# The first pass of a two-layer attention kernel: another way to spread c, another order of its side work, more buffers

## The chip, the cores and the metric

The kernel runs on one core of a Trainium2 chip. The metric is the device time in microseconds (us) of one execution. The engines are TensorE (PE, with its weight loads listed apart as PEld), VectorE (DVE), ScalarE (ACT), GpSimd (POOL) and SyncE (SP). SP issues every transfer of this kernel, in one queue, in order; all transfers run on 16 shared DMA engines. Each engine works through its own instructions in the order in which the program was laid out, and waits for semaphores of the others.

## The reference

The reference is an encoder of two layers over 1024 tokens of width 1024. Each layer normalizes x, scales and shifts it by values that come from a vector c, projects it, attends, gates and adds. What matters here is the start of layer 0:

```python
mod = jax.nn.silu(c) @ ada_w + ada_b
shift, scale, gate = jnp.split(mod[:, None, :], 3, axis=-1)
h = _rmsnorm(x, norm_g[0]) * (1.0 + scale) + shift
proj = h @ w_in
q, k, v, z = jnp.split(proj, [DA_WIDTH, 2 * DA_WIDTH, 3 * DA_WIDTH], axis=-1)
q = _rope(q, positions); k = _rope(k, positions)
```

`_rope` needs the sines and cosines of positions times 32 frequencies. All products are kept near float32: each operand is split into a high part (float32r) and the rest, and three products are added (`mm3`).

## The kernel before, in words

Tokens come in 8 tiles of 128, and the 1024 features in 8 chunks of 128. The **first pass** takes the first 512 tokens (tiles 0 to 3, `xs0`), chunk by chunk (the loop over `k` at L610). For a chunk it needs three things.

- The modulation of the 128 features: shift (`modb`) and scale (`moda`) are dot products of silu(c) with rows of `ada_ss0`. `load_c` (L421) loads c into all 128 partitions with one broadcast transfer, ACT makes tanh (L427), DVE makes 2 silu(c) (L428), and ACT copies it to the PSUM tile `cb` (L559). A chunk has two `ada` tiles of 512 KB (`ada0`, L561) and two DVE products with sums (`mod_dot`, L434); L442 makes `moda` final. Four `ada` buffers go round (`ADA_B`).
- The transposed chunk of x. ACT and DVE take the squares of the four tiles (`sq_x`, L527), one `inv_rms` (L465, with a power on POOL at L171) serves all four, and then the tiles are scaled in place: the first 256 columns on ACT (L567), the other 768 on DVE (L621), behind the first modulation. `h_chunk` (L479) lets PE transpose the four 128x128 blocks (L488), ACT writes `h0h` (L493) and the unrounded `h` (L495), POOL writes the rest `h0l` (L498).
- The split weights of v: `load_wv` (L542) fetches `wvr`, ACT rounds it (L547), POOL takes the rest (L548). Each four chunks there is also a strip of the weights of k (`wk0`, split in `split_raw`, L229 and L230). A strip waits in one of two `wraw` buffers.

PE then runs 15 products of 128x512 for the chunk (L638 to L644): 12 for four v accumulators (`vacc`), 3 for the first k accumulator (`kacc`). With `SKEW` 1 the transposes of the next chunk stand among them. Amid the last chunks the x of tokens 512 to 1023 (`xs1`) and the first strips of q (`wq0`) are loaded, after `ada` of chunk 7. Behind the last modulation stand `angles` (L572): ten DVE instructions and three sines on ACT, whose results go to DRAM (`tabS`, L594) and come back as `cosT` and `sinT` (L599).

After the pass come the q product of the first half (`qacc`, L648) and `store_v` (L359), which splits a v accumulator into a `v_hl` buffer (two of them, `VB`) and sends it to DRAM; only then is its PSUM bank free. Then the **second half** of the tokens follows with the same weights, then k and q of head 0, the second half of v's columns (`v0_tile`), and the attention. During these, DVE also works off the modulation of layer 1 (`gen_mods`, L453), with `ada` tiles that SP loads between the others.

The order on each engine is laid out by a scheduler from the program's order and its own estimates; `tc.issue_after(ins)` pins what a block issues behind `ins` on that engine.

Of the kernel before, what the change touches and what calls it, by code (L numbers as in the profile page):

```python
# [60 lines left out]
VB = (2, 3)  # L61
# [3 lines left out]
WQ_AT = 6  # L65
# [3 lines left out]
X_CUT = 256  # L69
FIN_LAG = 1  # L70
# [15 lines left out]
def trunk(ctx: ExitStack, tc: tile.TileContext, A, out):  # L86
# [329 lines left out]
    def mod_load(src, mp, nb, tag="ada"):  # L416
        w = mp.tile([P, D], F32, name="ada", tag=tag, bufs=nb)
        SP.dma_start(w, src)
        return w

    def load_c(pl, th, **kw):  # L421

        c2 = pl.tile([P, D], F32, name="c2", **kw)
        SP.dma_start(c2, A["c"].to_broadcast([P, D]))

        def fin():
            S.activation(th, c2, AF.Tanh, scale=0.5)  # L427
            V.scalar_tensor_tensor(out=c2, in0=th, scalar=1.0, in1=c2, op0=ALU.add, op1=ALU.mult)  # L428

        return c2, fin  # L430
# [48 lines left out]
    def h_chunk(l, xn4, k, dst, hp, sub=G, wide=False, act=False, f32=None):  # L479
# [13 lines left out]
        S.activation(hh, tr[:, :n, :], AF.Identity, bias=bk, scale=ak)  # L493
        if act:
            S.activation(tmp, tr[:, :n, :], AF.Identity, bias=bk, scale=ak)  # L495
# [18 lines left out]
    def load_x(half):  # L514

        xs = []
        for j in range(4):
            if half == 1 and j > 1:
                xs.append([wp.tile([P, HF], F32, name="xth", tag="rp", bufs=6) for _ in range(2)])
            else:  # L520
                xs.append([p1.tile([P, D], F32, name="xt", tag="xt", bufs=6)])
            for i, x_ in enumerate(xs[j]):
                n = D // len(xs[j])
                SP.dma_start(x_, A["x"][half * 4 + j, :, i * n : i * n + n])
        return xs

    def sq_x(xs, on_act=range(4)):  # L527
        ss = sm.tile([P, 4], F32, name="xss")
        for j, x_ in enumerate(xs):
            for i, piece in enumerate(x_):  # L530
                dst = ss[:, j : j + 1] if i == 0 else sm.tile([P, 1], F32, name="xs2")
                if j in on_act:
                    junk = p1.tile([P, D], BF16, name="junk", tag="junk", bufs=1)
                    S.activation(junk[:, : piece.shape[1]], piece, AF.Square, accum_out=dst)
                else:
                    junk = p1.tile([P, D], BF16, name="junk2", tag="h32", bufs=2)
# [24 lines left out]
    def ada0(j):  # L561
        return [mod_load(A["ada_ss0"][j, i], p1, ADA_B) for i in range(2)]
# [1280 lines left out]
```

## Time and profile before

| what | us |
|---|---|
| three runs, median (lowest to highest) | 1440.93 (1437.67 to 1443.14) |
| the profiled execution, its own time | 1438.65 |
| its span, first to last instruction | 1436.9 |
| PE busy in the span | 1388.8 |
| DVE, ACT, POOL busy | 917.5, 728.7, 610.6 |

The span leaves 1.75 us of the profiled execution's time outside. A row of the timeline gives the start, the duration, the engine, the line, the operation, output and inputs, sizes and count, and in brackets the idle time of the engine before it with what ended it. Rows of several instructions are merged (x4). The end of a PE product is modelled and overlaps the start of the next: the pace of PE is read from starts. A row of the windows gives, for a stretch, its length and the busy time and count of PE, PEld, DVE, ACT and POOL, then the granted PE clock (1.00 is full), the share of the DMA engines in use and their GB/s. A row of waits gives who waited for whom, the total, the times, and the longest.

### The profile page before, as it was taken

The numbers are of one execution on the slowest core, as the hardware profiler recorded it, in microseconds if no ns is written. First come the engines' busy times: TensorE is split into PE (matmuls) and PEld (weight loads), VectorE is DVE, ScalarE is ACT, GpSimd is POOL, SyncE is SP. The second block draws the span as 40 slices with busy tenths as digits, with TensorE's granted clock in tenths as the row PEclk, the third lists the DMA queues.
The fourth block names the chain that finished last, engine by engine and source line by source line (L and its number), as shares of the span: only waits on it lengthen the run. The fifth ranks groups of instructions, "written<-read, shape, count | busy, mean of one in ns | idle before, by whom it ended". The sixth has DMA issues, their size and how long they took to land. (4 is left out here: it accounts for less than half of the span.)

```text
span 1436.9 us, 20644 instructions
## 1 busy us (share of the span) xinstructions
PE 1388.8 (97%) x7388; PEld 1158.8 (81%) x7388; DVE 917.5 (64%) x1372; ACT 728.7 (51%) x1287; POOL 610.6 (42%) x483
## 2 busy tenths in 40 slices
PE   5999999999999999998999999999999999999997
PEld 4778788888888888887787877887888888888886
DVE  6656877767777767677435985545666555555355
ACT  5622375666565656566343452335455554545342
POOL 4416164656464646464461343532141331412572
PEclk9999999999999999999999999999999999999999
DMA  8787723333332333237653145398343432336563
GB/s 326 238 254 237 255 70 93 84 104 81 96 101 84 96 89 91 86 96 248 236 183 125 38 132 184 122 305 236 133 130 111 130 101 77 104 96 217 185 237 136
DMA packets 135527, 213.70 MB, mean 149 GB/s; under 512 B 19072, under 2 KB 56064, under 8 KB 135424
## 3 DMA queue, kind: packets, MB, share of 16 engines
q1 hardware_dynamic: 135424, 212.38, 47.1%
q8 instruction: 58, 0.95, 0.3%
q14 instruction: 45, 0.37, 0.1%
HBM read 137.92 MB, written 50.80 MB: 131 GB/s over the span
## 5 line engine op out<-in xcount | busy, mean ns | idle before, releaser
L384 ACT CAST pth<-tr 128x512 fp32r<-128x512 f32 x256 | 150.6, 588 | 284.2 <-PE tr L382 281.9
L399 DVE TENSOR_REDUCE nm<-s 128x1 f32<-128x1024 f32 x192 | 234.1, 1219 | 77.2 <-PE s L773 65.7
L385 DVE TENSOR_TENSOR ptl<-tr,pth 128x512 fp32r<-128x512 f32 x256 | 176.2, 688 | 139.4 <-ACT pth L384 138.9
L230 POOL TENSOR_TENSOR wl<-wraw,wh 128x512 fp32r<-128x512 f32 (+2 forms) x79 | 103.6, 1314 | 205.6 <-ACT wh L229 183.4
L401 ACT ACTIVATE e<-s,nm 128x1024 f32<-128x1024 f32 x128 | 143.7, 1123 | 29.8 <-DVE nm L399 29.2
L382 PE MATMUL tr<-ident,e 128*128 128x128 f32 x1024 | 155.1, 274 | 2.3 <-DVE ptl L385 2.0
L382 PEld LDWEIGHTS tr<-ident,e 128*128 128x128 f32 x1024 | 121.2, 140 | 43.6 <-DVE ptl L385 19.2
L184 PE MATMUL acc<-h0h,wh 128*128 128x512 f32 x360 | 150.1, 417 | 1.9 <-DVE v_hl L362 1.8
L184 PE MATMUL pv<-pth,vt 128*128 128x256 f32 x512 | 147.1, 287 | 0.0
L185 PE MATMUL pv<-ptl,vt 128*128 128x256 f32 x512 | 145.8, 285 | 0.0
L186 PE MATMUL pv<-pth,vt 128*128 128x256 f32 x512 | 144.7, 283 | 0.0
L186 PE MATMUL acc<-h0h,wl 128*128 128x512 f32 x360 | 143.1, 398 | 0.5 <-POOL wl L230 0.5
L185 PE MATMUL acc<-h0l,wh 128*128 128x512 f32 x360 | 142.0, 394 | 0.0
L1013 POOL TENSOR_TENSOR wol<-wor,woh 128x512 fp32r<-128x512 f32 x64 | 85.0, 1351 | 84.7 <-ACT woh L1012 77.2
L185 PEld LDWEIGHTS pv<-ptl,vt 128*128 128x128 f32 x512 | 97.6, 191 | 2.9
L184 PEld LDWEIGHTS pv<-pth,vt 128*128 128x128 f32 x512 | 97.4, 190 | 2.9 <-ACT pth L384 0.2
L186 PEld LDWEIGHTS pv<-pth,vt 128*128 128x128 f32 x512 | 97.6, 191 | 0.1
L326 POOL TENSOR_TENSOR rp_r<-rp_raw,cosT 128x512 f32<-128x512 f32 x38 | 49.8, 1311 | 91.0 <-ACT rp_raw L321 50.8
L331 POOL TENSOR_TENSOR rp_sw<-rp_sw,sinT 128x512 f32<-128x512 f32 x42 | 55.4, 1318 | 74.1 <-DMA rp_sw<-rp_raw 73.9
L773 PE MATMUL s<-ks,qa 128*128 128x512 f32 x256 | 82.6, 404 | 2.8 <-DVE e L781 2.6
L781 DVE SCALAR_TENSOR_TENSOR e<-s,z,e 128x1024 f32<-128x1024 f32 x64 | 82.1, 1283 | 2.1
L773 PE MATMUL s<-ks,qb 128*128 128x512 f32 x256 | 81.1, 395 | 0.0
(590 smaller groups left out, 3335.4 us busy)
## 6 DMA issues: line engine op xcount, KB each, us to landing
ada<-in_ada_ss SPq DMA_DIRECT2D x32, 512.0 KB, 6.0
wraw<-in_w_s SPq DMA_DIRECT2D x64, 256.0 KB, 2.9
vS<-v_hl SPq DMA_DIRECT2D x32, 512.0 KB, 5.9
vt<-vS SPq DMA_DIRECT2D x32, 512.0 KB, 3.7
wor<-in_w_out SPq DMA_DIRECT2D x64, 256.0 KB, 3.9
rp_sw<-rp_raw SPq DMA_DIRECT2D x168, 64.0 KB, 2.0
bc_s<-bc_d SPq DMA_DIRECT2D x34, 256.0 KB, 4.1
oS<-bc_s SPq DMA_DIRECT2D x30, 256.0 KB, 2.5
```

The lines of the kernel that those rows point to most:

```text
L184: PE.matmul(psum, ah, bh, start=first, stop=False)
L185: PE.matmul(psum, ah, bl, start=False, stop=False)
L186: PE.matmul(psum, al, bh, start=False, stop=last)
L230: sub = (V if pair_of else G).tensor_sub(l_[:, :n], raw[:, :n], f32v(h_[:, :n]))
L382: PE.transpose(tr[:, j, :], p[:, kt * P : (kt + 1) * P], ident)
L384: mk["S"] = S.copy(pth[kh][:, :, dst], tr).ins
L385: mk["V"] = V.tensor_sub(ptl[kh][:, :, dst], tr, f32v(pth[kh][:, :, dst])).ins
L399: mk["V"] = V.reduce_max(nm, s_ps, axis=AX.X, negate=True).ins
L401: mk["S"] = S.activation(e, s_ps, AF.Exp, bias=nm, scale=1.0, accum_out=zs).ins
L773: PE.matmul(s_ps[:, kc * HF : (kc + 1) * HF], src[:, c, ql], KS[h][kc][:, c, :], start=fst, stop=not fst)
L781: combined.append(V.scalar_tensor_tensor(out=e0, in0=e1, scalar=z1[:, 0:1], in1=e0, op0=ALU.mult, op1=ALU.add).ins)
L1013: in_turn(G.tensor_sub(lo, raw, f32v(hi)))
```

## The change

- **c.** One row of c is loaded into one partition (`crow`); tanh and the product run on this partition; two float32 products of a row of ones with it write `cb`, spread over all partitions. `crow` and `th` both take `ada` buffers. `c2`, which the modulation of layer 1 needs in SBUF, is copied from `cb` amid chunk 5.
- **Products of ones.** Before the spread 8, and behind it 28 products of `ones` with itself (128x128, float32) are issued on PE into a bank of the `acc` rotation (`warm`), and not used.
- **Last token tile apart.** Squares, mean and scale of tiles 0 to 2 are made first; tile 3 has its own chain, with its squares half on ACT and half on DVE. DVE scales tiles 0 to 2 without being pinned behind the first modulation.
- **Angles and sines.** `positions` is loaded after the weights of chunk 1. The DVE steps of the angles stand in four parts behind the modulations of chunks 1 to 4, the sines behind `h_chunk` of chunks 4 and 5, the last two DVE steps and the transfers at chunk 6.
- **Order.** The splits of weights are pinned behind the `h` of the chunk before; the q strips are fetched one chunk earlier (`WQ_AT` 5), behind `ada` of chunk 6; `xs1` behind `ada` of chunk 7. Squares of `xs1`: the first two tiles on DVE, the other two on ACT.
- **Buffers.** `v_hl` of layer 0 has four buffers instead of two; `dynamic_dma_scratch_size` is 1024 instead of its default.

```diff
-VB = (2, 3)
+VB = (4, 3)
-WQ_AT = 6
+WQ_AT = 5
+WARM = (8, 28)
+SIN_AT = (4, 5, 6)
...
+    warm = bank("acc", "warm")
+    def keep_busy(n):
+        for _ in range(n):
+            PE.matmul(warm[:, 0:P], ones, ones, start=True, stop=True)
+    crow = p1.tile([P, D], F32, name="crow", tag="ada", bufs=ADA_B)
     th = p1.tile([P, D], F32, name="cth", tag="ada", bufs=ADA_B)
-    c2, c_fin = load_c(p1b, th)
-    xs0 = load_x(0)
+    SP.dma_start(crow[0:1, :], A["c"])
+    xs0 = [load_x(0, 0)]
+    xs0 += [load_x(0, j) for j in range(1, 4)]
+    keep_busy(WARM[0])
...
-    c_fin()
-    cb = bank("cb", "cb", [P, D])
-    S.copy(cb, c2)
...
+    c_act = S.activation(th[0:1, :], crow[0:1, :], AF.Tanh, scale=0.5).ins
+    c_last = V.scalar_tensor_tensor(out=crow[0:1, :], in0=th[0:1, :], scalar=1.0, in1=crow[0:1, :], op0=ALU.add, op1=ALU.mult).ins
+    cb = bank("cb", "cb", [P, D])
+    for f in range(2):
+        fs = slice(f * HF, f * HF + HF)
+        spread = PE.matmul(cb[:, fs], ones[0:1, :], crow[0:1, fs], start=True, stop=True).ins
+    with tc.issue_after(spread):
+        keep_busy(WARM[1])
...
-    y0 = inv_rms(sq_x(xs0, X_ACT0), 4)
+    y_ = inv_rms(ss0[:, 0:3], 3)
+    for j in range(3):
+        y0[j] = y_[:, j : j + 1]
+        S.mul(xs0[j][0][:, :X_CUT], xs0[j][0][:, :X_CUT], y0[j])
+    sq_halves([xs0[3][0][:, :HF], xs0[3][0][:, HF:]], ss0[:, 3:4])
+    y0[3] = inv_rms(ss0[:, 3:4], 1)[:, 0:1]
+    h_chunk.act = S.mul(xs0[3][0][:, :X_CUT], xs0[3][0][:, :X_CUT], y0[3]).ins
...
+    for j in range(3):
+        x_rest(j)
...
+    def sines(n):
+        with tc.issue_after(h_chunk.act):
+            if n == 0:
+                S.activation(kk, ang, AF.Sin, scale=0.5)
+                S.activation(nsin, ang, AF.Sin, scale=-1.0)
+            if n == 1:
+                S.activation(ang, ang, AF.Sin)
+                S.copy(c2, cb)
...
+            if k >= 0:
+                with tc.issue_after(m_last):
+                    next(angle_steps, None)
         if k < 0:
             with tc.issue_after(m_last):
-                for j in range(4):
-                    V.tensor_scalar(xs0[j][0][:, X_CUT:], xs0[j][0][:, X_CUT:], y0[:, j : j + 1], None, op0=ALU.mult)
-        if k == KT - 1:
-            with tc.issue_after(m_last):
-                angles()
+                x_rest(3)
         if k == X1_AT:
-            xs1 = load_x(1)
+            with tc.issue_after(mod_load.last):
+                xs1 = [load_x(1, j) for j in range(4)]
         if k == WQ_AT:
-            wq0 = load_strip([A["w_s0"][0, 0, f] for f in range(2)], [4, 4], None, ada_pair)
+            with tc.issue_after(mod_load.last):
+                qraw = fetch_strip([A["w_s0"][0, 0, f] for f in range(2)], [4, 4])
+            with tc.issue_after(h_chunk.act):
+                wq0 = split_strip(qraw, None, ada_pair)
             q_split = load_strip.last
         if 0 <= k < KT:
             h_chunk(0, xs0, k, h0[k][0], p1, act=True)
+            if k + 1 < KT:
+                with tc.issue_after(h_chunk.act):
+                    wv0.append(split_wv(vraw))
+            if k in SIN_AT:
+                sines(SIN_AT.index(k))
...
-    norm_x(sq_x(xs1), xs1)
+    ss1 = sm.tile([P, 4], F32, name="xss")
+    with tc.issue_after(m_last):
+        for j in range(2):
+            sq_piece(xs1[j][0], ss1[:, j : j + 1], False)
+    with tc.issue_after(h_chunk.act):
+        for j in range(2, 4):
+            sx = sm.tile([P, 1], F32, name="xs2")
+            sq_piece(xs1[j][0], ss1[:, j : j + 1], True)
+            sq_piece(xs1[j][1], sx, True)
+            V.tensor_add(ss1[:, j : j + 1], ss1[:, j : j + 1], sx)
+    norm_x(ss1, xs1)
...
-    nc = bacc.Bacc("TRN2", target_bir_lowering=False, num_devices=1)
+    nc = bacc.Bacc("TRN2", target_bir_lowering=False, num_devices=1, dynamic_dma_scratch_size=1024)
```

More of the change, by code (lines that the diff above doesn't have):

```diff
@@ L417, in mod_load @@
         w = mp.tile([P, D], F32, name="ada", tag=tag, bufs=nb)
-        SP.dma_start(w, src)
+        mod_load.last = SP.dma_start(w, src).ins
         return w
[L421 to L430, printed above, removed]
     def mod_dot(w, bias, acc, c_):
@@ L512, in trunk @@
     p1 = pool(st1, "p1a")
-    def load_x(half):
-        xs = []
-        for j in range(4):
[L518 to L536, printed above, removed]
-                    V.tensor_tensor_reduce(out=junk, in0=piece, in1=piece, scale=1.0, scalar=0.0, op0=ALU.mult, op1=ALU.add, accum_out=dst)
-                if i:
-                    V.tensor_add(ss[:, j : j + 1], ss[:, j : j + 1], dst)
-        return ss
```

106 lines of the change are left out of this document (76 added, 30 removed).

## The prediction

> **What bounds the kernel now.** I read the page first, then the waits of PE, then the timeline of the first 60 us, then windows.
>
> ```profile
> span 1436.9 us, 20644 instructions
> ```
>
> The waits of PE over the first 60 us:
>
> ```profile
> PE trh L488 <- ACT xt L567: 14.5, 1, 14.5
> PE vacc L643 <- POOL h0l L498: 2.1, 1, 2.1
> ```
>
> PE does not start before 14.5 us, and has one more long wait, near the end of the first pass. The kernel's time is that of PE, so what the first pass can give is this start, this wait, and what both cost in pace. The timeline of the start:
>
> ```profile
> 0.72 0.39 SPq L150 DMA_DIRECT2D vec<-in_vec  x1
> ...
> 1.17 0.42 SPq L424 DMA_DIRECT2D c<-in_c  x1
> ...
> 2.46 0.15 DVE L162 TENSOR_SCALAR g<-vec 128x1 f32<-128x1 f32 x1 [1.47 <-DMA vec<-in_vec]
> ...
> 6.22 1.06 ACT L427 ACTIVATE cth<-c 128x1024 f32<-128x1024 f32 x1 [4.22 <-DMA c<-in_c]
> 7.31 1.23 DVE L428 SCALAR_TENSOR_TENSOR c<-cth,c 128x1024 f32<-128x1024 f32 x1 [4.70 <-ACT cth L427]
> ...
> 10.08 1.06 ACT L534 ACTIVATE junk<-xt 128x1024 bf16<-128x1024 f32 x1 [0.49 <-DMA xt<-in_x]
> ...
> 11.23 1.23 DVE L537 CUSTOM_DVE_ANT_0 junk<-xt 128x1024 bf16<-128x1024 f32 x1 [1.22 <-DMA xt<-in_x]
> ...
> 12.57 0.17 DVE L466 TENSOR_SCALAR xss<-xss 128x4 f32<-128x4 f32 x1
> ...
> 12.87 1.28 DVE L434 CUSTOM_DVE_ANT_0 ada<-ada,cb,vec 128x1024 f32<-128x1024 f32 x1
> ...
> 15.52 4.26 DVE L621 TENSOR_SCALAR xt<-xt,rq_y 128x768 f32<-128x768 f32 x4
> ...
> 17.01 0.80 PE L638 MATMUL vacc<-wvh,h0h 128*128 128x512 f32 x1 [0.87 <-ACT h0h L493]
> ...
> 18.87 1.05 PE L488 MATMUL trh<-ident,xt 128*128 128x128 f32 x4
> ...
> 22.21 0.16 DVE L442 SCALAR_TENSOR_TENSOR moda<-moda,vec 128x1 f32<-128x1 f32 x1
> ...
> 23.30 0.50 PE L638 MATMUL vacc<-wvh,h0h 128*128 128x512 f32 x1 [0.18 <-ACT h0h L493]
> ```
>
> x of the third tile lands at 10.08, of the fourth at 11.23. From L466 at 12.57 DVE works without a gap until `moda` of chunk 1 at 22.37 (22.21 + 0.16), 9.8 us, and the products of chunk 1 follow at 23.30, 0.93 later. So chunk 1 is set by DVE; that chunk 0 runs at half pace (0.80 a product) hides behind that. From there PE runs on:
>
> ```profile
> 46.74 0.39 PE L638 MATMUL vacc<-wvh,h0h 128*128 128x512 f32 x1
> ...
> 48.78 0.39 PE L641 MATMUL kacc<-h0h,wl 128*128 128x512 f32 x1
> 51.28 1.93 PE L643 MATMUL vacc<-wvh,h0l 128*128 128x512 f32 x4 [2.10 <-POOL h0l L498]
> ...
> 53.73 0.79 PE L184 MATMUL acc<-h0h,wq 128*128 128x512 f32 x1
> ...
> 55.06 0.39 PE L184 MATMUL acc<-h0h,wq 128*128 128x512 f32 x1
> ```
>
> Six chunks from 23.30 to 46.74 are 3.91 us each. Of chunk 7 the first ten products took 2.04 (46.74 to 48.78), 0.227 each. Without the stall its 15 products would end at 50.15; the q product starts at 53.73, and its first three take 1.33 instead of 0.68. The stall costs 3.6 + 0.65 = **4.2 us**, twice its 2.1 of idle, since PE comes back slow. The windows show this in the granted clock:
>
> ```profile
> 50.00:55.00 5.00, 3.62 (x8) 2.37 (x9) 2.07 (x4) 3.84 (x11) 1.22 (x1) 0.66 0.71 213
> ```
>
> Why `h0l` was late stands on ACT: the table load of the sines and two sines stand between `h0h` and `h` of chunk 7.
>
> ```profile
> 47.20 1.28 ACT L588 ACT_TABLE_LOAD   x1
> ...
> 49.12 0.76 ACT L495 ACTIVATE h<-trh,modb,moda 128x512 f32<-128x512 f32 x1
> ```
>
> **The change part by part.** *The start.* The traffic in windows:
>
> ```profile
> 1.50:4.50 3.00, 0.00 (x0) 0.00 (x0) 0.15 (x1) 0.50 (x1) 0.00 (x0) 1.00 0.78 183
> ...
> 6.50:14.50 8.00, 0.04 (x1) 0.04 (x1) 5.50 (x9) 4.65 (x8) 1.04 (x1) 1.00 1.03 416
> ```
>
> The broadcast of c writes 524 KB (0.524 MB) and goes ahead of x. At the 416 GB/s of the second stretch that is 1.26 us; at the 183 of the first, where the DMA engines were in use for 0.78 of the time, 2.87. I take 2.2: the first stretch is where c moved, but some of it is the start itself. So x of tile 2 lands at 7.9, its squares end 1.15 later as before (10.08 to 11.23), at 9.05, and DVE's run may start there, since tile 3 no longer stands ahead: 3.5 earlier than 12.57. The run has the same two modulations and four scalings, and about 1.0 more for tile 3 (half of the 1.23 of L537, one addition, a second L466, an estimate from these rows), and up to 0.4 of waiting for the first `ada` tile. **Start: 3.5 - 1.0 - 0.4 = 2.1 us** (1.2 with 1.26 for c; 3.2 with 2.87 and no waiting). Whether DVE scales tiles 0 to 2 or makes the modulation first moves chunk 0, not chunk 1.
>
> That c itself is sooner: its row is issued at 1.17 and lands as `vec` did (issued 0.72, used 2.46), near 2.9; tanh 1.06 and the product 1.23 end near 5.4, not 8.54. PE spreads from 5.5. The trace has no such spread. The nearest are products of ones late in the kernel:
>
> ```profile
> 1350.48 1.05 PE L830 MATMUL rb<-dg,ones 128*128 128x128 f32 x8
> ```
>
> Four float32 products of the program stand here as 8 rows, so 0.26 us each at full pace; transposes at slow pace (18.87, 1.05 for 4) are twice as long a row, 0.52. The spread is 8 such widths: 2.1 to 4.2 us. The 28 products behind it are 7.4 to 14.7. They end at 15.0 at full pace (hidden: before, DVE was done with the modulation of chunk 0 at 15.5), and at 24.4 at slow pace. The transposes of chunk 0 stand behind them on PE, and ACT's `h0h`, POOL's `h0l` behind these. I take the fast end, because the first 8 products have by then kept PE at work from about 1 us; the slow end is a rival. TensorE: Matmul & The Clock Gate in the Trainium skill (Part 1) says that about 3.4 us of activity lifts the gate to full pace and an idle window takes it back; by that the 28 run fast. The trace agrees as far as it goes: PE is slow at 17.01 and 18.87, and at full pace for the chunks from 23.30 on. By the slow row alone the start would give nothing.
>
> With `crow` and `th` in `ada` buffers, the loads for chunk 1 wait for the spread's end; 416 GB/s of x and `ada` of chunk 0 are queued ahead, so 0.
>
> *Angles and sines.* DVE's steps cost what they did, now between modulations.
>
> ```profile
> 43.89 1.39 DVE L575 CAST ang<-posi 128x256 f32<-128x256 int32 x1
> ```
>
> A chunk has 2.7 of DVE (two of 1.28 and L442) in 3.91 us of PE, so later ones cover theirs. The cast stands between the modulations of chunks 1 and 2, when DVE is just ahead: 0 to 0.6 lost, I take 0.2. On ACT the table load and two sines come to 2.1 in one chunk; ACT's own work there is a rounding and two activations like L495's 0.76, about 2.2. 4.3 against 3.91 is 0.4 late at most, and I take 0: ten of a chunk's products (2.3 us) stand ahead of the first that needs `h0l`. The stall of 4.2 goes. ScalarE: Activation LUTs in the Trainium skill (What ACT_TABLE_LOAD costs) gives 2.66 us with a drain; the trace shows 1.28, with the sine at once behind it. By the page ACT would be 1.8 late and PE lose a few tenths.
>
> What is late next is `vacc`: the q product takes a bank that `store_v` must free, an ACT copy and a DVE subtraction:
>
> ```profile
> 52.58 0.69 DVE L362 TENSOR_TENSOR v_hl<-vacc,v_hl 128x512 fp32r<-128x512 f32 x1 [2.89 <-ACT v_hl L361]
> ...
> 95.98 0.59 ACT L361 CAST v_hl<-vacc 128x512 fp32r<-128x512 f32 x1 [1.61 <-DMA vS<-v_hl]
> ```
>
> From the last product into the bank to its end took 2.0 (51.28 to 53.27); five products at 0.227 cover 1.15. That leaves 0.8 (0 if another bank is free, 1.6 behind a square of `xs1` on ACT). **End of the pass: 4.2 - 0.8 = 3.4** (2.6 to 4.2). The squares of `xs1` now on DVE (1.23 each) lie beside the q product (24 x 0.227 = 5.5 us); without that cover they would cost 2.5.
>
> *Order of loads.* The second q strip needs the `wraw` buffer of the second k strip, which POOL frees late:
>
> ```profile
> 37.75 1.30 POOL L230 TENSOR_TENSOR wl<-wraw,wh 128x512 fp32r<-128x512 f32 x1 [0.79 <-ACT wh L229]
> ```
>
> If SP waits there, `ada` and `wvr` of chunk 7 and all of `xs1` queue behind it. I take 0.3 for this (0 if SP issues `ada` first; the price at worst is a rival). Moving `positions` takes 0.3 us of traffic (128 KB at 416 GB/s) from ahead of `ada`; counted with the start.
>
> *More buffers.* After the pass:
>
> ```profile
> SPq L364 <- DVE v_hl L362: 12.5, 1, 12.5
> ```
>
> ```profile
> 63.00:73.00 10.00, 10.00 (x54) 8.05 (x54) 6.75 (x10) 5.43 (x8) 7.27 (x6) 1.00 0.12 48
> 74.00:110.00 36.00, 34.01 (x146) 26.84 (x145) 19.67 (x32) 9.94 (x17) 4.45 (x3) 1.00 0.91 269
> ```
>
> SP stood 12.5 us behind a `v_hl` that had no buffer, with the DMA at 0.12; then the loads ran late, ACT waited for stores (95.98), and PE lost 2.0 (36.00 - 34.01) up to 110. With four buffers the third and fourth tile are stored at once. I take 1.5 of these 2.0; the bounds are 2.0 and -1.0, since `warm` shifts the turn of PSUM banks by one and a k product may wait for the last store (0.59 + 0.69) instead of the first. All transfers are SP's, so the smaller scratch counts 0.
>
> **Sum:** 2.1 + 3.4 - 0.2 - 0.3 + 1.5 = **6.5 us**. The profiled execution takes 1438.65, 2.3 under the median; taken from it 1432.1, taken from the median **1434.4**.
>
> **Rivals.** *More is gained.* Start 3.2, end 4.2, later waits 2.0, nothing given back: 9.4, 1431.5. For it: c's stretch is slow at 183 GB/s, and the later waits share one cause. Against: each term at its bound.
>
> *Given back at chunk 7.* SP waits for POOL as in the row, shifted by the start: 39.05 - 2.1 = 37.0. The `ada` loads:
>
> ```profile
> ada<-in_ada_ss SPq DMA_DIRECT2D x18, 512.0 KB, 6.3
> ```
>
> They land at 43.3; modulation 2.7 and 0.93 more: products from 46.9, where 46.74 - 2.1 = 44.6 was wanted. 2.3 of stall and, as after the stall of 2.1, 1.9 of slow pace: 6.5 - 4.2 = 2.3, **1438.6**. For it: one queue, two buffers. Against: POOL has slack to free the buffer sooner.
>
> *Slower.* The 28 products run slow and end at 24.4. Transposes 1.05, then 0.93 to the products at 26.4; chunk 0 at half pace again 6.3 (17.01 to 23.30): chunk 1 at 32.7, 9.4 later. End and later terms remain (4.4): 5.0 slower, **1445.9**. It decides from where the products end: past 15.5 they eat the start, past about 19.4 the kernel is slower, and with the products a third slower than the transposes' row it is 1450. For it: nothing here shows such a stream at full pace this early. Against: it needs PE to stay slow through 20 us of work.
>
> **How the numbers follow.** Forecast 0.48 (its own range 1432 to 1437), more gained 0.26, given back 0.12, slower 0.14. 0.5%, about what a measurement of this kernel can tell from no change, is 7.2 us, 1433.7. Of the forecast's 0.48 I put 0.20 below that. The slower rival passes 1448.1 only in its worse half, 0.08; its other 0.06 is no change that can be told. Faster 0.20 + 0.26 = 0.46; same 0.28 + 0.12 + 0.06 = 0.46; slower 0.08. The range leaves out the slower rival and a little below: 1428.5 to 1441.5.
>
> **What would show it.** Start: products of chunk 1 near 21.2, with `x` of tile 2 near 7.9; the 28 products ending before 16. End: no wait of L643 for `h0l`, q product near 49.5, granted clock 1.00 there. Buffers: no 12.5 us wait of SP for `v_hl`, PE idle under 1 between 60 and 105. Wrong if chunk 1 starts no earlier, if chunk 7 waits for `moda`, or if PE's gain at 110 us is gone further on.

## The result, and the profile after

The changed kernel takes 1444.12 us (median of 13 runs, 1441.98 to 1448.72), the kernel before 1441.72 in the runs beside it (13 runs, 1437.67 to 1444.26). The ratio is 1.0024 [1.0013, 1.0035]: some 3.5 us slower by the ratio, 2.4 by the medians, and above the range forecast. The profiled execution takes 1443.97; its span is 1442.1. PE is busy for 1402.3 us instead of 1388.8, but 76 of its rows are the products of ones and the spread.

To see where the time went, PE's products are counted without those 76 rows (7388 in both traces) and the starts of equal numbers compared. A *lead* below zero is earlier than before. The profiled execution of before took 1438.65, 3.1 us under its median, and the changed one is near its own; leads toward the end are therefore against a fast execution, and come out larger than the ratio. In the changed kernel it is +0.6 us at the 40th product (chunk 1), +2.6 at the 143rd (chunk 7), -0.3 at the 167th (in the q product), -3.2 at the 420th to the 600th (113 to 154 us), **+3.8 at the 760th** (195 us) and +4.9 at the end. So 3 us were won, and 7 lost within 40 us.

The start, from the timeline after:

```profile
5.04 1.98 PE L595 MATMUL cb<-crow,ones 1*128 1x512 f32 x4 [0.22 <-DVE crow L591]
...
6.95 8.14 PE L551 MATMUL warm<-ones 128*128 128x128 f32 x56
...
8.62 1.06 ACT L520 ACTIVATE junk<-xt 128x1024 bf16<-128x1024 f32 x1 [2.10 <-DMA xt<-in_x]
...
10.43 0.16 DVE L457 TENSOR_SCALAR xss<-xss 128x3 f32<-128x3 f32 x1
...
11.59 1.68 DVE L614 TENSOR_SCALAR xt<-xt,rq_y 128x768 f32<-128x768 f32 x3 [0.62 <-POOL rq_y L173]
...
15.78 0.61 DVE L614 TENSOR_SCALAR xt<-xt,rq_y 128x768 f32<-128x768 f32 x1
...
17.08 0.62 ACT L231 CAST wh<-wraw 128x512 fp32r<-128x512 f32 x1 [3.28 <-DMA wraw<-in_w_s]
...
17.61 0.77 ACT L484 ACTIVATE h0h<-trh,modb,moda 128x512 fp32r<-128x512 f32 x1
...
18.43 0.79 PE L698 MATMUL vacc<-wvh,h0h 128*128 128x512 f32 x1 [2.90 <-ACT h0h L484]
...
18.83 0.24 DVE L433 SCALAR_TENSOR_TENSOR moda<-moda,vec 128x1 f32<-128x1 f32 x1
...
24.34 0.47 PE L698 MATMUL vacc<-wvh,h0h 128*128 128x512 f32 x1
```

x of tile 2 lands 1.5 us sooner, the products of ones end at 15.09, and `moda` of chunk 1 is done at 19.07, 3.3 earlier than before. PE has nothing of this here. On ACT the rounding of the first k strip, which now stands ahead of `h0h`, waits 3.28 for its transfer; PE idles 2.9, comes back at half pace, and chunk 1 starts at 24.34, 1.0 later than before. That is not so in every execution: of the seven other profiles with this same start, four have the products of ones end near 17, an idle of only 0.87 and chunk 1 at 22.6 to 22.9, ahead of before's 23.30 (e5, e6, e7, e9; the last section shows the reason).

Chunk 7 is late, from the timeline of SP, DVE and PE, and from the waits of SP from 28 to 45 us:

```profile
33.28 4.13 SPq L210 DMA_DIRECT2D wraw<-in_w_s  x2
38.34 0.33 SPq L533 DMA_DIRECT2D wvr<-in_w_v  x1
38.72 0.42 SPq L636 DMA_DIRECT2D tabS<-nsin  x1
39.68 0.33 SPq L636 DMA_DIRECT2D tabS<-ang  x1
41.48 0.33 SPq L533 DMA_DIRECT2D wvr<-in_w_v  x1
41.91 0.85 SPq L420 DMA_DIRECT2D ada<-in_ada_ss  x2
...
45.54 1.28 DVE L425 CUSTOM_DVE_ANT_0 ada<-ada,cb,vec 128x1024 f32<-128x1024 f32 x1 [2.94 <-DMA ada<-in_ada_ss]
...
49.18 0.50 PE L698 MATMUL vacc<-wvh,h0h 128*128 128x512 f32 x1 [1.72 <-ACT h0h L484]
...
54.00 0.50 PE L186 MATMUL acc<-h0h,wq 128*128 128x512 f32 x1 [1.13 <-DVE v_hl L364]
```

```profile
SPq L533 <- POOL wvl L543: 3.3, 4, 1.4
SPq L210 <- POOL wl L232: 3.0, 1, 3.0
...
SPq L636 <- ACT ang L629: 0.5, 1, 0.5
```

The q strip's transfers (33.28) wait 3.0 us for POOL. Behind them two `wvr` transfers wait for POOL to free their buffers (0.9 and 1.4), the stores of the sines wait 0.7 for ACT, and only at 41.91 are the `ada` tiles of chunk 7 issued (34.36 before). The wait for `h0l` is gone, the q product waits 1.13 for a bank, and it starts at 54.00, where it was 53.73.

The stretch that decides is later. The waits of PE from 140 to 200 us, before and after:

```profile
PE acc L184 <- DVE v_hl L362: 1.1, 1, 1.1
PE s L773 <- DVE e L781: 0.2, 1, 0.2
```

```profile
PE acc L186 <- DVE v_hl L364: 3.8, 1, 3.8
PE s L845 <- DVE e L853: 2.1, 1, 2.1
```

The window from 150 to 165 us, before and after:

```profile
150.00:165.00 15.00, 13.66 (x60) 10.69 (x59) 12.89 (x21) 4.18 (x7) 0.00 (x0) 1.00 0.86 280
```

```profile
150.00:165.00 15.00, 9.15 (x36) 6.99 (x35) 14.03 (x22) 2.88 (x7) 0.00 (x0) 0.78 0.84 273
```

PE's busy time falls from 13.66 to 9.15, its clock to 0.78, and DVE is full, with 14.03. DVE's order there, before and after:

```profile
156.58 1.28 DVE L434 CUSTOM_DVE_ANT_0 ada<-ada,c,vec 128x1024 f32<-128x1024 f32 x1
...
158.92 0.68 DVE L362 TENSOR_TENSOR v_hl<-vps,v_hl 128x512 fp32r<-128x512 f32 x1
...
161.51 1.28 DVE L434 CUSTOM_DVE_ANT_0 ada<-ada,c,vec 128x1024 f32<-128x1024 f32 x1 [0.18 <-DMA ada<-in_ada_g]
...
162.90 0.68 DVE L362 TENSOR_TENSOR v_hl<-vps,v_hl 128x512 fp32r<-128x512 f32 x1
```

```profile
159.89 1.28 DVE L425 CUSTOM_DVE_ANT_0 ada<-ada,c,vec 128x1024 f32<-128x1024 f32 x1 [0.32 <-DMA ada<-in_ada_g]
...
161.26 1.28 DVE L425 CUSTOM_DVE_ANT_0 ada<-ada,c,vec 128x1024 f32<-128x1024 f32 x1
...
162.48 1.28 DVE L364 TENSOR_TENSOR v_hl<-vps,v_hl 128x512 fp32r<-128x512 f32 x2
```

Here layer 1's last modulations and the eight products of the first layer's gate (`gen_gate`, one 512 KB `ada` tile each) are worked off while PE makes the products for the second half of v's columns and for the first softmax. PE needs from DVE the subtractions that free v's banks (`v_hl`) and the combination `e`. After the change both `v_hl` of the last v tiles stand behind all eight gate products. Before, one of the two stood behind six of them, at 158.92, and only the other behind all eight, at 162.90; PE lost 1.1 there.

### The profile page after: what moved, and what is told of

Same layout as the page of the kernel before. It is cut to its first block, busy times and chain, and to the rows that moved or that the text cites. A ratio compares the mean times of both kernels' runs of the same rounds, so it can differ in the third digit from the quotient of the medians.

```text
span 1442.1 us, 20782 instructions
## 1 busy us (share of the span) xinstructions
PE 1402.3 (97%) x7464; PEld 1173.4 (81%) x7464; DVE 925.6 (64%) x1378; ACT 724.6 (50%) x1285; POOL 611.6 (42%) x484
## 5 line engine op out<-in xcount | busy, mean ns | idle before, releaser
L188 PEld LDWEIGHTS acc<-h0h,wl 128*128 128x128 f32 x360 | 68.2, 189 | 16.2 <-POOL wl L232 0.9
```

What stands on the lines that cost most here:

```text
L188: PE.matmul(psum, al, bh, start=False, stop=last)
```

## The experiments

All kernels are the changed one with the edit shown, unless it says "before". The table gives the lead (us, against the profiled execution of before) at a few products, and the ratio of the time to before. A lead is from one execution; the row "again" is a second profile of the changed kernel and shows how far that repeats (at the 143rd product, in chunk 7, the two differ by 2.2 us).

| kernel | 40th | 100th | 143rd | 167th | 600th | 760th | end | ratio |
|---|---|---|---|---|---|---|---|---|
| changed | +0.6 | +0.4 | +2.6 | -0.3 | -3.2 | +3.8 | +4.9 | 1.0024 [1.0013, 1.0035] |
| e16 again | +0.4 | +0.3 | +4.8 | +1.5 | -1.3 | +4.7 | +3.7 | 1.0018 [1.0005, 1.0031] |
| e1 late | 0.0 | -0.2 | +2.4 | -0.1 | -2.3 | +1.1 | +2.7 | 1.0009 [0.9996, 1.0022] |
| e2 VB 2 | +1.9 | +1.7 | +6.8 | +3.6 | +8.1 | +9.0 | +9.4 | 1.0033 [1.0021, 1.0045] |
| e3 k0 | -2.1 | -0.6 | +2.4 | -0.3 | -2.2 | +4.2 | +7.0 | 1.0039 [1.0023, 1.0055] |
| e4 before, VB 4 | -0.2 | -0.2 | -0.2 | +0.4 | +3.0 | +3.6 | +4.4 | 1.0017 [1.0006, 1.0028] |
| e5 pin | -1.0 | -0.2 | +6.0 | +3.6 | +0.3 | +1.3 | +3.5 | 1.0001 [0.9987, 1.0016] |
| e6 gate1 | -1.1 | -0.6 | +4.8 | +1.6 | -0.8 | +2.3 | +9.0 | 1.0007 [0.9992, 1.0022] |
| e7 WQ 6 | -0.9 | -0.4 | -0.3 | -0.9 | -1.8 | +2.8 | +6.1 | 1.0021 [1.0005, 1.0036] |
| e8 all | -2.1 | -1.0 | -0.9 | +0.5 | -0.3 | 0.0 | +1.2 | 0.9992 [0.998, 1.0003] |
| e9 no gate | -1.1 | -0.2 | +4.8 | +1.6 | -0.7 | -2.4 | -0.7 | 0.998 [0.9965, 0.9995] |
| e10 one ada pair | -1.7 | +0.4 | +0.5 | +1.6 | +4.0 | +1.5 | +2.8 | 0.9999 [0.9985, 1.0013] |
| e11 gate on POOL | -1.9 | +0.4 | +4.3 | +1.1 | -2.3 | +4.4 | +5.7 | 1.0024 [1.0009, 1.0038] |
| e12 moda on ACT | -1.4 | -0.5 | +5.2 | +2.7 | +1.2 | +4.4 | +3.6 | 1.0037 [1.0017, 1.0057] |
| e13 no angles | +0.2 | +0.8 | +4.6 | +2.0 | -1.0 | +5.5 | +4.4 | 1.0022 [1.0009, 1.0035] |
| e14 moda, pin | +0.2 | +0.3 | +4.2 | +1.6 | -0.2 | +1.6 | +1.9 | 1.0011 [1.0, 1.0022] |
| e15 no sines | -2.1 | -1.5 | +1.7 | -0.7 | -2.8 | +4.0 | +3.3 | 1.0031 [1.0019, 1.0043] |

The stretch at 150 to 165 us is called the *wall* below, and what PE loses in it is the difference between the columns 600th and 760th. Taken together the profiles say more than any one of them. Five kernels have both stores of the last v tiles behind all eight gate products on a full DVE (changed, e16, e3, e13, e15): they lose 6.0 to 7.0. In three the scheduler laid one of the two stores ahead of one to three of them (e6, e7, e12): 3.1 to 4.6. In the four with these stores in their own buffers and all gate work on DVE (e1, e5, e8, e14) both stand ahead of the last gate products: 0.3 to 3.4. In e10 both stand behind all eight, but these are done by 159.9, and PE, 4.0 behind, waits for nothing there.

**First set.** Theory S: the time is lost at 150 to 165 us because the stores of the last v tiles stand behind the gate products in VectorE's queue. Rival W: the transfers of that stretch are the wall, whatever the order. Rival B: the bank that the products of ones take shifts the turn of the PSUM banks, and that makes the wait.

e1_late, the last two stores into their own buffers instead of gate slots:

```diff
-        if tt < V_LATE:
-            store_v(0, p1b, acc, tt, fh)
-        else:
-            store_v(0, pm, acc, tt, fh, "ada", 3)
+        store_v(0, p1b, acc, tt, fh)
```

> The changed kernel, with the v_hl tiles of the last two v tiles (tokens 768 to 1023, second half of v) in the four v_hl buffers instead of the ada buffers. On DVE both stores then stand ahead of the last gate products instead of behind all of them. Theory S (7 us are lost at 155 to 163 because these two stores stand behind the gate products on DVE, so that the next products find no PSUM bank): no wait of PE for v_hl over 1 us there, PE ahead of the kernel before by about 3 us at 170 us, and 1437 to 1439, 0.997 to 0.998 of before. Rival W (the gate weights land when they land, so PE stands until about 163 in any order): PE waits on, a wait of 2 us or more stays between 150 and 165, 1442 or more, ratio 1.000 or more.

The loss from the 600th to the 760th product falls from 7.0 to 3.4 us, and the ratio by 0.0015 (2 us; the intervals overlap). What is left is 2.67 us of waiting for `e`, from its timeline of PE:

```profile
160.85 0.85 PE L842 MATMUL s<-ks,qa 128*128 128x512 f32 x2 [2.67 <-DVE e L850]
```

S holds for half of the loss: the wait for `v_hl` is down to 0.3. But the numbers put down for S (3 us ahead at 170 us, ratio 0.997 to 0.998) did not come, and W's (a wait of 2 us or more, ratio 1.000 or more) did. This run alone doesn't separate the two.

e2_vb2 (`VB = (2, 3)` again) and e4_b_vb4 (before with `VB = (4, 3)` and the scratch of 1024):

> The changed kernel with two v_hl buffers again, all else as changed. DVE's order around 150 to 165 is then that of the kernel before. Theory S: the 7 us of loss are gone with the order, but SP stands over 10 us behind v_hl again and the waits from 85 to 110 are back: 1440 to 1443, ratio 0.999 to 1.000. Rival B (the bank that the products of ones take shifts the turn of the PSUM banks, and that makes the wait): the wait of 3.8 us for v_hl stays, ratio 1.002 or more.

> The kernel before with four v_hl buffers and the smaller scratch, nothing else of the change. Theory S: SP's wait of 12.5 us for v_hl is gone, PE is 2 to 3 us ahead by 150 us, and then the stores of the last two v tiles stand behind gate products on DVE: 4 us or more of waiting between 150 and 170, ratio 1.000 to 1.003. If the buffers alone were a gain and the loss came from the first pass: ratio 0.998.

Without the buffers the changed kernel is slower still by its ratio (1.3 us, with overlapping intervals); chunk 7 is later, a wait for `v_hl` of 2.27 us returns at 92.55, and the lead at the 600th is +8.1. So four buffers carry the gain of the second half in this layout. Its wall is small, 0.9 (8.1 to 9.0): with two buffers the scheduler lays the stores between the gates as in before, and PE comes to it 11 us later than in the changed kernel; the run doesn't part these two. The wait for `v_hl` in the wall is 1.9, not the 3.8 of rival B, and the ratio is above what S had. In the kernel before the same edit gains 1.6 us at the 380th product and gives back 5 by the 400th, waiting for weights and a copy at 106 to 109 us. S had expected a lead of 2 to 3 us and then 4 us or more of waiting there; it was a loss of 3.0 and 2.3 of waiting, so only the ratio lay in its range. What the buffers are worth depends on the rest of the layout.

e3_k0, the split of the first k strip behind `h_chunk` of chunk 0:

```diff
+                if k:
                     with tc.issue_after(h_chunk.act):
                         for d_, w_ in zip(wk0, split_strip(kraw)):
                             d_ += w_
...
             h_chunk(0, xs0, k, h0[k][0], p1, act=True)
+            if k == 0:
+                with tc.issue_after(h_chunk.act):
+                    for d_, w_ in zip(wk0, split_strip(kraw)):
+                        d_ += w_
```

> The changed kernel with the split of the first k strip behind the activations of chunk 0 on ACT. Theory H (the start gained nothing because that split, waiting for its weights until 17.08, stood ahead of h0h of chunk 0): h0h starts near 16.0, PE idles about 1.3 instead of 2.9 ahead of chunk 0, products of chunk 1 start 1 to 2.5 us earlier than in the changed kernel (24.3). Rival: chunk 1 is set by DVE or by the clock alone, and stays within 0.5 us. In both theories DVE's order at 155 to 163 stays, and by S the gain of the start is lost there: 1443 to 1445, ratio 1.001 to 1.003; without S it is 1.0005 to 1.0015.

PE's first product waits 0.87 instead of 2.90 and runs at full pace, and chunk 1 starts at 21.72, 1.6 before before's. That is near the start that was predicted (21.2). It holds where the spread runs at the faster of its two paces: the six profiles with this edit and that pace have chunk 1 at 21.6 to 22.3, against 23.7 to 25.7 in the four without the edit. In the two with the edit and the slower pace (e13, e14) the products of ones end near 17.4, the transposes stand behind them, and chunk 1 comes at 23.95, later than the 22.6 to 22.9 of the four without the edit. And in e3 nothing is left of the gain at the 167th product, the wall takes 6.4, and the kernel is not faster (1.0039, above the 1.001 to 1.003 expected). The three waits that give it back, from its timeline of PE:

```profile
38.38 0.66 PE L479 MATMUL trh<-ident,xt 128*128 128x128 f32 x4 [0.85 <-ACT h L486]
48.94 0.50 PE L703 MATMUL vacc<-wvh,h0h 128*128 128x512 f32 x1 [2.36 <-ACT h0h L484]
53.98 0.50 PE L186 MATMUL acc<-h0h,wq 128*128 128x512 f32 x1 [1.31 <-DVE v_hl L364]
```

**Second set: the wall, and chunk 7.** e5_pin is e1_late, and the last three gate products, whose tiles are loaded as before, are pinned behind the last store:

```diff
+    with tc.issue_after(store_v.last):
+        for j in range(KT - 3, KT):
+            mod_dot(g3[j - KT + 3], part("ada_bg0")[:, j : j + 1], gcol[:, j : j + 1], c2)
```

> The changed kernel with the stores of the last two v tiles in their own buffers (as in e1_late), and the products of the last three gate rows held behind the store of the last v tile; their loads are issued as before. Theory D (VectorE's order: stores and softmax of 150 to 165 us stand behind gate products, which wait for their loads): PE's waits for v_hl and e between 140 and 200 us together below 2 us (5.9 in the changed kernel, 3.0 in e1_late), granted clock above 0.9 from 155 to 170, 620th product within 1 us of before's or earlier; ratio to before 0.998 to 1.000. Theory W (the transfers of this stretch are the wall, whatever VectorE's order): the same products wait at the same place as in e1_late, ratio 1.001 or above.

```profile
150.00:165.00 15.00, 13.90 (x64) 11.21 (x63) 13.94 (x23) 3.48 (x6) 0.00 (x0) 1.00 1.03 323
```

```profile
161.34 0.70 PE L844 MATMUL s<-ks,qa 128*128 128x512 f32 x2 [1.10 <-DVE e L852]
```

The loss from the 600th to the 760th falls to 1.0, at clock 1.00 from 150 to 165, with 2.4 us of waiting (below 2 was expected). But e5 comes to the wall 2.6 us later than e1_late (+0.3 against -2.3), waits for `e` until 161.34 where e1_late waited until 160.85, and leaves at +1.3 against +1.1. So the run doesn't show whether the pin or the later coming made the loss smaller, and alone it doesn't refute W: W's place held, and its ratio (1.001 or above) is inside the interval. The work and the number of loads are those of e1_late; one gate load comes a store later in SP's queue.

e6_gate1, all gate products from the first tile:

```diff
         for j in range(KT):
-            mod_dot(load(A[f"ada_g{l}"][j]), part(f"ada_bg{l}")[:, j : j + 1], gcol[:, j : j + 1], c2)
+            if j == 0 or l:
+                wg = load(A[f"ada_g{l}"][j])
+            mod_dot(wg, part(f"ada_bg{l}")[:, j : j + 1], gcol[:, j : j + 1], c2)
```

> The changed kernel with all eight gate products of the first layer made from the first gate tile, so that seven loads of 524 KB are left out (the gate is then not the reference's); the eight products stay. If the loads of the gates are what the stores wait for through VectorE's queue, the last gate product ends before 155 us (162.5 in the changed kernel), PE's waits between 140 and 200 us fall below 1 us (5.9), and the 640th product starts 2 to 4 us before before's (4.2 after it in the changed kernel): ratio 0.995 to 0.998. If the products themselves fill VectorE (8 of 1.28 us), the waits stay above 3 us and the ratio is 1.001 or above.

```profile
150.00:165.00 15.00, 11.79 (x47) 9.06 (x46) 14.96 (x25) 3.38 (x6) 0.00 (x0) 0.92 0.34 100
```

The DMA share from 150 to 165 us is down from 0.84 to 0.34, and DVE is full all the same (14.96 of 15): the last gate product ends at 163.7. PE waits 3.2 us. So the gate loads aren't the wall, which speaks against W; DVE's work is (no wait from 147.5 us on). Both kernels start this run of work behind a wait for the tile of layer 1's last modulation (2.5 us, until 144.76, in the changed kernel; 2.6 us, until 147.51, in e6), and no experiment takes that wait away. (The +9.0 at the end comes from stretches past 500 us: the profiled execution, 1448.13, is the slowest of its ten, whose median is 1441.19.)

e7_wq6 (`WQ_AT = 6`):

> The changed kernel with the first q strip fetched in chunk 6 again, as before the change (chunk 5 now). If chunk 7 is late because SP waits at that fetch for the raw buffer: no wait of SP over 5 us before 42 us, chunk 7's first product within 0.5 us of before's 47.4 (2.55 late now), and the pass ends 1 to 2.5 us earlier, or the wait moves to the q product at 51 to 54 us and nothing is gained. Because the second half is walled in at 150 to 165 us, little of it is left at the end: ratio 1.000 to 1.002.

Chunk 7 is on time (-0.3), as expected of SP's queue. But then the transposes of the second half, which PE has ahead of the q product, wait for the scaled rows of `xs1`:

```profile
51.05 0.30 PE L479 MATMUL trh<-ident,xt 128*128 128x128 f32 x1 [1.03 <-DVE xt L468]
52.83 0.33 PE L479 MATMUL trh<-ident,xt 128*128 128x128 f32 x1 [1.36 <-DVE xt L468]
```

e8_all, the edits of e1, e3, e5 and e7 together:

> All mends at once: e5_pin with the first k strip split behind the first chunk's transposes (e3_k0) and the q strip fetched in chunk 6 (e7_wq6). Theory D with both starts mended: chunk 1 near 21.7 us (24.3 in the changed kernel), no stall at chunk 7, 300th product 2 to 4 us before before's, wall below 2 us: ratio 0.996 to 0.999. If what is won at the start is always given back at the next transfer: ratio equal to e5_pin's within 0.001.

Chunk 1 is near 21.7 (21.64) and chunk 7 doesn't stall, but `xs1` takes the lead (-0.9 to +0.5 at the 167th); the wall costs 0.3. Its ratio is 0.3% under the changed kernel's, and their intervals don't overlap: this is the best evidence that the mended places together made the loss (0.998 to 1.0003 against 1.0013 to 1.0035). It can't be told from before, its lead at the 300th product is +1.3 instead of the 2 to 4 ahead that were expected, and it is within 0.001 of e5_pin, as the alternative had it: what is won at the start is given back.

**Third set: what fills VectorE.** e9_nogate leaves the gate out; e11_pool_k0 is e1 and e3 with every second gate product on POOL and ACT:

```diff
+            if l == 0 and j % 2:
+                G.tensor_mul(w, w, c2)
+                S.activation(w, w, AF.Identity, scale=0.5, accum_out=o_)
+            else:
+                mod_dot(w, b_, o_, c2)
```

> The changed kernel without the first layer's eight gate products and their loads (the gate column is zero, so the output is not the reference's). Theory D2 (VectorE is full from 148 to 165 us: eight products of 1.28 us, and PE's stores and softmax stand in the same queue): without them PE's waits between 140 and 200 us fall below 1.5 us (5.9 in the changed kernel), the clock stays at 1.00 from 155 to 170, and the 640th product starts 2.5 to 4 us before before's: ratio 0.995 to 0.998. Theory P (the place is a wall for another reason, the strips' transfers or the banks): the 640th product is still later than before's, ratio 1.000 or above.

> e1_late and e3_k0 together, and every second gate product of the first layer made on POOL (a product of 128x1024, some 2.7 us by twice the rows of 128x512) and summed on ACT, so that VectorE has four products fewer (5.1 us) between 148 and 165 us. Theory D2: PE's waits between 140 and 200 us below 1.5 us, clock 1.00 there, the 640th product 1.5 to 2.5 us before before's (where it stood at the 600th): ratio 0.997 to 1.000. If POOL's and VectorE's work disturb each other, or the products are late and hold the three tiles: waits above 3 us, ratio 1.001 or above.

Without the gate the wall is not only gone, PE gains 1.7 us there (-0.7 to -2.4), waiting 0.5 at full clock; the ratio is at the upper end of what theory D2 gave, while the 640th product, at -1.8, is not the 2.5 to 4 us ahead that it gave. The window, without the gate:

```profile
150.00:165.00 15.00, 14.54 (x66) 11.70 (x65) 6.08 (x11) 5.31 (x11) 0.00 (x0) 1.00 0.55 175
```

This is the one kernel here that is faster than before, and it leaves work out, products and loads both; e6, which leaves out seven of the eight loads alone, is the one that parts them. With half of the products on POOL the 640th product is at -2.2, as D2 said, but at the 660th the lead is +4.3: ACT, too, works in order, and the exponential of the softmax stands behind a sum that waits for POOL's product, whose tile came late.

```profile
171.07 1.22 PE L856 MATMUL s<-ks,qa 128*128 128x512 f32 x2 [4.17 <-ACT e L403]
```

The same mistake as in the changed kernel, on another engine; waits and ratio are those of the rival, that the products are late.

e10_ada1_k0, e3_k0 with one pair of `ada` tiles for all modulations of the pass (`wm = wm0`):

> e3_k0 with all sixteen modulation products of the first pass made from the first pair of tiles, so that fourteen loads of 524 KB are left out of the first 45 us (the output is not the reference's). Theory T (transfers set the end of the first pass, so what is won at its start is given back): the start is as in e3_k0 (20th product 20.5 to 22.0), chunk 7 does not stall, and the 167th product starts at 52 to 55 us instead of 57.6. Rival Q (SP's queue or POOL's splits hold chunk 7 and the q product, not the bytes): the 167th product stays above 56.5 us. The rest is walled in at 150 to 165 us by theory D2, so the whole gains at most 2 us against e3_k0: ratio 1.000 to 1.004.

Theory T falls: with the DMA share at 0.2 to 0.4 from 25 to 45 us the 167th product is later still (59.4, where 57.6 was e3's). Chunk 7 is only 0.5 late; then PE waits 2.78 for `xs1`, among whose squares DVE has a modulation of layer 1 that waits for its own tile.

**Fourth set: the lead of the first pass.** e12_moda_k0 is e3_k0 with L433 on ACT, e13_noang_k0 leaves out the angle steps, e14_best is e12 with the order of e5:

```diff
-        mod_dot(ws[1], bsc[:, js], a_[:, js], c_)
-        return V.scalar_tensor_tensor(out=a_[:, js], in0=a_[:, js], scalar=1.0, in1=g[:, js], op0=ALU.add, op1=ALU.mult).ins
+        return mod_dot(ws[1], bsc[:, js], a_[:, js], c_).ins
+    def mod_fin(l, j):
...
+        S.activation(a_[:, js], a_[:, js], AF.Identity, bias=g, scale=g)
```

> e3_k0 with the last step of each modulation (a 128x1 product and sum, L433) moved from VectorE to ACT. Theory V (VectorE paces the chunks: its modulations, the angle pieces and the 128x1 steps, each of which waits until POOL's running product has ended, come to more than PE's 4.0 us a chunk): VectorE has idle time again between 20 and 40 us (4.9 of 5 busy in e3_k0), and the lead won at the start is kept longer: 100th product at least 1.5 us before before's (0.64 in e3_k0). Rival L (the loads pace the chunks): VectorE then waits for ada tiles, 100th product as in e3_k0 within 0.4 us. Chunk 7 still waits for SP's queue in both, and 150 to 165 us are as in e3_k0, so the ratio is 1.002 to 1.005.

> e3_k0 with the range reduction of the angles left out (the angles are zero, so the output is not the reference's; the sines and their table load stay). It shows what the pieces amid the chunks cost VectorE. Theory V: the 100th product at least 1.2 us before before's (0.64 in e3_k0), and L433's mean falls or rises with where it meets POOL. If the pieces lie in idle time of VectorE, the 100th product is as in e3_k0 within 0.3 us. Ratio 1.002 to 1.005 by both, since the walls at chunk 7 and 150 us stay.

> e12_moda_k0 with e5_pin's order of the gates: the start mended, VectorE relieved in the chunks, and the stores and softmax of 150 to 165 us ahead of the last gates. Theory V with D2: 300th product 0.5 to 2 us before before's, PE's waits between 140 and 200 us below 2.5 us at clock 1.00, 760th product within 1 us of before's; ratio 0.997 to 1.000. If the first pass gives its lead back at chunk 7 in any case: as e5_pin, 1.000.

Theory V falls. In e12 DVE has idle time from 30 to 40 us (busy 3.17 and 2.76 of 5) and in e13 from 25 on, yet from the 60th to the 100th product they lose 0.9 and 0.7 us (1.4 in e3), and chunk 7 is later than in e3. Rival L had its number: e12's 100th product is at -0.5 (-0.6 in e3), and DVE waits 2.10 for an `ada` tile at 35.30. But e10, without these loads, loses 1.8 over the same products, so the loads alone aren't the pace either. e13 and e14 had the slower spread and so the later start; their leads can't be set against e3's. e14, with the q strip in chunk 5 and chunk 7 late, is at 1.0011 and loses 1.8 at the wall.

e15_nosin_k0 leaves the table load and sines out:

> e3_k0 with ACT's table load and three sines left out (VectorE copies the angles in their place, 0.4 us; the tables are angles, so the output is not the reference's). Theory A (with VectorE freed in e12 and e13 the lead still went at 35 to 39 us, and what stands there is the table load and two sines, 2.0 us of ACT ahead of the rounding of the next chunk): the 100th product at least 1.5 us before before's if the run starts as e3_k0 did (20th product 1.6 ahead), or loses less than 0.3 us between the 60th and the 100th (1.4 in e3_k0). Otherwise it loses above 0.8 there. Chunk 7 is late in any case, since SP's queue is the same; ratio 1.001 to 1.005.

> The changed kernel itself, a second profile, to see which of its steps repeat: by all theories chunk 7 late by 2 us or more, the lead of 2 to 4 us at the 600th product, and the wall after it (640th product 2.5 us or more after before's). The pace of the spread at 5 us (1.98 us for four products in the first profile, 3.78 in six others with the same code there) may be either.

In e15 the loss from the 60th to the 100th is 0.5 (from -2.05 to -1.53), and the first number of theory A is met. By this pair most of the 1.4 was ACT's table load and two sines ahead of the next `h0h`; but kernels with the same table load there lost from 0.7 (e13) to 2.0 (e11), so one profile each gives the size only roughly. e16 repeats the steps: the late chunk 7 (4.8 instead of 2.6), a lead at the 600th (-1.3 instead of -3.2, less than the 2 to 4 expected), the wall (6.0 instead of 7.0).

## Why the prediction was wrong, by its steps

- **Start, 2.1.** "Chunk 1 is set by DVE": the step failed in that I moved the splits on ACT without asking what they wait for. ACT's rounding waited for a transfer ahead of `h0h`, with 2.9 us of PE's idle and the slow clock after it. Undone (e3), chunk 1 is 1.6 earlier than before, in executions with the faster spread. DVE's chain was 3.3 us faster, more than forecast, and that is luck: its run began at 10.43, 2.1 earlier instead of 3.5 (x came 1.5 sooner instead of 2.2), but the four scalings took 2.29 instead of 4.26, which the sum had as unchanged. Before, they stood beside POOL's products; the last section shows what that can cost.
- **Clock.** The products of ones ended at 15.09, as said, but not "at full pace": from 5 to 10 and from 10 to 15 us the granted clock was 0.82 and 0.84, and 56 rows took 8.14 where e16 took 6.52. A full pace better than priced and a stretch of half clock cancelled. The rival "slower" had that products which end past 15.5 eat the start, and that holds: in e5 they end near 17, and chunk 1 is 0.6 ahead of before instead of 2.1. That the pace stays slow to 24.4 did not come: in e5 full clock begins at 12.6. What the prediction did not price is that products which end early leave PE idle behind them; in the changed kernel that cost more (chunk 1 is 1.0 later).

```profile
5.00:10.00 5.00, 4.96 (x23) 3.71 (x24) 1.43 (x3) 2.43 (x5) 0.00 (x0) 0.82 0.97 379
10.00:15.00 5.00, 5.00 (x40) 5.00 (x40) 4.31 (x11) 2.81 (x7) 2.69 (x3) 0.84 1.04 413
```

- **Order of loads, 0.3.** It was the rival "given back at chunk 7", which I gave 0.12. SP waits for POOL until 37.05, as priced there (37.0); the later waits for POOL's `wvl` (2.3) and for ACT at the sines' stores (0.7), which the sum had not put in SP's queue, add to it: `ada` of chunk 7 was used at 45.5 instead of 43.3. With the strip later (e7) chunk 7 is on time and `xs1` late.
- **Angles, 0.2, and sines, 0.** The cover held in the changed kernel, which had no lead to lose (+0.6 at the 60th product, +0.4 at the 100th). In e3, which had one, the table load and sines cost about 0.9 (1.4 less 0.5, from one profile each).
- **End, 3.4.** The mechanism was right in each part: no wait for `h0l`, 1.13 for a bank (0.8 forecast). But the stall of chunk 7 took its place, so the 4.2 us were not won. Up to the q product the sum had 5.0; it was 0.3, or a loss of 1.5 in the second profile.
- **Buffers, 1.5.** Right in this layout, and too small: from the 167th to the 420th product PE won 3.0 (2.8 again). SP's 12.5 us wait is gone. That it is so anywhere else is not shown: in the kernel before, e4 lost 2.6 over the same products.
- **Past 110 us** the sum had no term. This is the step that decided the sign: a lead of 3.2 was taken as kept to the end. The prediction named its loss only as what would make it wrong. The scheduler laid DVE anew, stores behind gates, and the full stretch of DVE cost 7.0 (6.0 again): 7.0 - 3.2 = 3.8. The losses by order (6.0 to 7.0, 3.1 to 4.6, 0.3 to 3.4) show the order, e9 the gate work. How the rest moves the end by another us either way (+1.1, and -1.0 again) stays open; both have a step of 1.2 at one transpose near 570 us.

## What to carry to other kernels

A gain on the engine that bounds is only worth what the next full stretch of another engine lets through: follow the lead past the edited stage to the end, and look for an engine near 100% in the windows there. Where a scheduler lays out the queues, any edit moves the order elsewhere; compare the order of instructions in each full stretch, and see to it that what the bounding engine waits for stands ahead of work that waits for transfers (here the buffers of e1_late did much of it; what a pin adds to them is not shown). On every engine, name what the moved instruction itself waits for, and what then stands behind it.

## What was not expected of the hardware

**VectorE waits for POOL.** Small DVE steps amid the chunks take up to eight times their time, and end when POOL's running product ends:

```profile
22.50 1.30 POOL L489 TENSOR_TENSOR h0l<-h,h0h 128x512 fp32r<-128x512 f32 x1 [0.85 <-ACT h L486]
...
23.03 0.79 DVE L433 SCALAR_TENSOR_TENSOR moda<-moda,vec 128x1 f32<-128x1 f32 x1
...
23.75 1.42 POOL L543 TENSOR_TENSOR wvl<-wvr,wvh 128x512 fp32r<-128x512 f32 x1
...
24.05 1.26 DVE L579 TENSOR_SCALAR kk<-kk 128x256 f32<-128x256 f32 x1
```

Their ends are 23.82 against 23.80, and 25.31 against 25.17. The first takes 0.16 with POOL at rest (at 15.71; 1.31 at the most, in e16), the second 0.29 (e12). The modulation products beside them (1.27, one input in PSUM) are not held. SBUF — State Buffer in the Trainium skill (Who interferes with whom) has the rule: a DVE operation with two SBUF inputs contends with a POOL operation that reads SBUF, one in a two-port mode with any POOL operation, and whoever is first keeps the other out for the whole instruction. The trace agrees. e12 and e13, which take such steps out of the chunks, show no gain for PE.

**The same products at two paces.** The four rows of the spread take 1.98 to 2.13 us in ten of the sixteen profiles with them and 3.77 or 3.78 in six (e5, e6, e7, e9, e13, e14), with the same code ahead of them. It is the granted clock. The first products of ones run at 0.24 us a row in all (16 rows in 3.78 in the changed kernel); 56 rows at full pace take 6.52 in e16, 0.12 a row. In the traces' clock records the first stretch at full clock begins at 3.9 to 5.4 us in the ten and at 12.4 to 13.6 in the six, so the spread runs at full pace in the ones and at half pace in the others. (The windows print 1.00 where a trace has no clock record yet.) Why it begins when it does stays open. The starts of e16 and of e5:

```profile
7.11 6.52 PE L551 MATMUL warm<-ones 128*128 128x128 f32 x56
...
18.16 0.50 PE L698 MATMUL vacc<-wvh,h0h 128*128 128x512 f32 x1 [4.09 <-ACT h0h L484]
```

```profile
4.96 3.78 PE L597 MATMUL cb<-crow,ones 1*128 1x512 f32 x4
8.67 8.36 PE L553 MATMUL warm<-ones 128*128 128x128 f32 x56
...
18.34 0.50 PE L700 MATMUL vacc<-wvh,h0h 128*128 128x512 f32 x1 [0.87 <-ACT h0h L486]
...
22.71 0.48 PE L700 MATMUL vacc<-wvh,h0h 128*128 128x512 f32 x1
```

The later clock leaves PE busy until `h0h` is nearly there. After the idle of 2.90, 4.09, 2.36 and 2.99 us (changed, e16, e1, e2) the clock records have half clock for 3.4 us or more, beginning at 17.8 to 19.1 us; after the 0.87 of e5, e6, e7 and e9 they have none until chunk 7. The length of the idle alone doesn't decide it: 2.69 us in e11 before chunk 0 and 2.36 in e3 before chunk 7 were followed by full clock.
